# A conv, FFN and attention trunk in split fp32: nine of eleven down pairs by seven products, the closing tile by tile, weight sums outside the layers

## The chip, the cores and the metric

The kernel runs on one core of a Trainium2 chip, as one program. The metric is device time in microseconds. The profile times five engines: PE (matrix products), DVE and ACT (elementwise work), POOL (elementwise work, and the queue that issues accumulating DMAs) and SP (the queue of plain loads).

## The reference

512 tokens of width 1024 go through one short-convolution layer, a SwiGLU layer, one sliding-window attention layer on shared K and V, and a second SwiGLU layer; each part is normed on both sides and added to the residual stream. Everything is fp32. What matters here is the SwiGLU:

```python
D_FF = ((8 * D_MODEL // 3 + 255) // 256) * 256      # 2816
def rmsnorm(x, g):
    xf = x.astype(jnp.float32)
    r = lax.rsqrt(jnp.mean(xf * xf, axis=-1, keepdims=True) + EPS)
    return (xf * r).astype(x.dtype) * g
def swiglu(h, w_gate_up, w_down):
    g, u = jnp.split(h @ w_gate_up, 2, axis=-1)
    return (jax.nn.silu(g) * u) @ w_down
```

## The kernel before

**Products.** An fp32 product is made of three products of rounded parts: each operand is split into a high part (an ACT copy, `whi` or `ahi`) and the remainder (a DVE subtraction, `wlo` or `alo`), and `mm3` (L181 to L183) multiplies low by high, high by high and high by low. A `raw` tile holds a loaded weight until it is split.

**Seven products.** The 22 feature tiles of the SwiGLU make 11 pairs. A gate pair is computed by a seven-product scheme of the Strassen-Winograd kind (class `Gates`, jobs p = 1 to 7; tiles `gx`, `gy`, `gz`). The down projection has two forms. `ROUNDS` divides the feature tiles: the pairs of each round but the last go by seven products as well (`down_jobs`; tiles `px`, `py`, `pz`; the results gathered into `mix` by DVE at L1057), and the last round's tiles are multiplied directly in the closing (`unit`; tile `pmix`). Before, the rounds are tiles 0 to 6, 6 to 10, 10 to 14 and 14 to 22: seven pairs by seven products, eight tiles directly.

**Sums of weights.** Four of the seven products of a pair take sums of weight blocks (t1 to t4 in the code). They are made in DRAM (tiles `hsum`) by DMAs on POOL's queue: four copies, two accumulates, then one and one more, in four steps (class `Sums`). `sum_on` (issued at L588) starts a set at the place that `BEGIN` names, and carries every started set one step further at each later place: c0 to c7 are the eight column blocks of the convolution, 0f1 to 0p10 places of the first SwiGLU, a0 to a7 of the attention, 1f1 of the second SwiGLU. h00 to h11 are sums for the gates, d00 to d12 sets for the down rounds (layer, round). The program keeps these DMAs in written order on POOL's queue, and a step is issued only once what it reads has landed.

**POOL's other work** stands in the same queue: the cuts and multiplications of the convolution (L701, L712), accumulates of gate weights onto `raw` tiles (L442), and the reciprocal roots of the norms (`ur`: L281 for the norm behind a layer, L303 for the norm ahead of the next).

**Opening and closing.** A layer's result is normed token tile by token tile (128 tokens each): `take` (from PSUM; its square by ACT, `junk` L250), `mean` (`uv` L277, `ur` L281), `scale` (by the gain, L273), `update` of the residual `h` (L286), `square` (L294), `mean2` (L299, L303), `norm` (`xn`, L308, by ACT). PE then turns xn (`xt`, L319). `last_tile` does the rest for the fourth tile while PE begins the next layer's gates, and `keep` places splits of later weights between. The closing before runs in two halves: all four tiles for the output's first 512 columns (`first_half`), then for the others (`second_half`), with splits of following weights (`ahead`, L405 and L410) between.

**Order.** Where `manual_schedule` is on, the instructions of an engine stand in written order. `Line` serves the split weights to the products: it fetches into at most 7 raw tiles and keeps at most 5 split weights (`N_RAW`, `N_W`).

## Time and profile before

| | us |
|---|---|
| median of three runs | 1044.0 (1043.23 to 1045.44) |
| the profiled execution | 1043.19 |
| its span | 1041.4 |
| PE busy in it | 1024.6 |
| DVE busy | 754.0 |
| ACT busy | 555.7 |
| POOL busy | 194.3 |

A timeline row reads: start, duration, engine, line, operation, out<-in, shapes, count, and in brackets the idle time before it with what ended that. Listed durations of matmuls overlap; the distance between two starts is what one costs.

### The profile page before, as it was taken

How to read it: one execution, taken by the hardware profiler on the slowest of the kernel's cores; microseconds unless marked ns; L12 is line 12 of the kernel's file. 1: busy time of each engine (PE TensorE's matmuls, PEld its weight loads, DVE VectorE, ACT ScalarE, POOL GpSimd, SP SyncE). 2: the span in 40 equal slices, each digit the busy share in tenths (PEclk: the TensorE clock that was granted, in tenths of full speed). 3: DMA queues.
4: the chain of work that ended last, by engine and by line, in shares of the span. 5: the costliest groups of instructions: out<-in, count | busy, mean ns of one | idle time of the engine just before them, and what ended most of it. 6: DMA issues, size and time to landing. Idle time of an engine off the chain costs nothing.

```text
span 1041.4 us, 17098 instructions
## 1 busy us (share of the span) xinstructions
PE 1024.6 (98%) x6652; PEld 930.0 (89%) x6652; DVE 754.0 (72%) x1190; ACT 555.7 (53%) x947; POOL 194.3 (19%) x231
## 2 busy tenths in 40 slices
PE   9999999998999999999999999999999999999997
PEld 7888888998989898999898888889998999989986
DVE  5775655886767788666578999689786688786654
ACT  7222224864655455454474777678565555545531
POOL 0242202130121111220132542022110101011001
PEclk9999999999999999999999999999999999999999
DMA  9667775899889888998335674378988878888802
GB/s 330 262 165 229 197 218 138 207 263 262 271 205 264 226 208 256 235 244 274 136 122 144 138 202 122 104 201 206 269 253 225 196 216 188 219 200 204 236 28 81
DMA packets 63825, 212.05 MB, mean 204 GB/s; under 512 B 6912, under 2 KB 7808, under 8 KB 59136
## 3 DMA queue, kind: packets, MB, share of 16 engines
q0 software_dynamic: 17728, 81.80, 39.6%
q1 hardware_dynamic: 45440, 128.51, 35.0%
q8 instruction: 52, 0.85, 0.3%
q10 hardware_dynamic: 576, 0.66, 0.2%
q14 instruction: 29, 0.24, 0.1%
HBM read 204.64 MB, written 44.04 MB: 239 GB/s over the span
## 4 chain that ended last, share of the span: by engine, by line
PE 80%; DVE 8%; DMA 4%; issue 4%; ACT 3%; POOL 1%; POOLq 0%; DVEq 0%; SPq 0%; ACTq 0%
PE gx L181 6%; PE gx L182 6%; PE gx L183 6%; DMA raw<-in_w_gb_dram 4%; PE pmix L181 4%; PE pmix L182 4%; PE pmix L183 4%; PE gz L181 3%; PE gz L183 3%; PE gz L182 3%; PE px L181 2%; PE px L182 2%; PE px L183 2%; DVE wlo L476 2%; PE pcub L660 2%
## 5 line engine op out<-in xcount | busy, mean ns | idle before, releaser
L476 DVE TENSOR_TENSOR wlo<-raw,whi 128x1024 fp32r<-128x1024 f32 x209 | 253.9, 1218 | 106.7 <-ACT whi L469 105.9
L469 ACT ACTIVATE whi<-raw 128x1024 fp32r<-128x1024 f32 x209 | 218.1, 1052 | 179.9 <-DMA raw<-in_w_gb_dram 66.4
L442 POOL DMA_DIRECT2D raw<-in_w_gb_dram x84 | 73.3, 877 | 465.9 <-DVE wlo L476 245.6
L181 PE MATMUL gx<-xt,whi 128*128 128x256 f32 x528 | 150.7, 285 | 4.8 <-ACT gr L955 3.7
L182 PE MATMUL gx<-xt,whi 128*128 128x256 f32 x528 | 150.0, 284 | 0.0
L183 PE MATMUL gx<-xt,wlo 128*128 128x256 f32 x528 | 149.9, 284 | 0.0
L181 PEld LDWEIGHTS gx<-xt,whi 128*128 128x128 f32 x528 | 102.0, 193 | 6.0 <-ACT gr L955 4.4
L182 PEld LDWEIGHTS gx<-xt,whi 128*128 128x128 f32 x528 | 102.0, 193 | 0.0
L183 PEld LDWEIGHTS gx<-xt,wlo 128*128 128x128 f32 x528 | 102.0, 193 | 0.0
L176 ACT ACTIVATE whi<-raw 128x1024 fp32r<-128x1024 f32 x31 | 32.8, 1058 | 58.9 <-PE pu L182 25.0
L181 PE MATMUL pmix<-wlo,ahi 128*128 128x512 f32 (+1 forms) x136 | 51.3, 377 | 0.0
L182 PE MATMUL pmix<-whi,ahi 128*128 128x512 f32 (+1 forms) x136 | 51.2, 377 | 0.0
L183 PE MATMUL pmix<-whi,alo 128*128 128x512 f32 (+1 forms) x136 | 51.2, 377 | 0.0
L177 DVE TENSOR_TENSOR wlo<-raw,whi 128x1024 fp32r<-128x1024 f32 x31 | 47.4, 1528 | 4.8 <-ACT whi L176 4.5
L181 PE MATMUL gz<-xt,whi 128*128 128x256 f32 x176 | 49.9, 284 | 0.8 <-DVE gr L934 0.8
L181 PE MATMUL gx<-x,whi 128*128 128x256 f32 x176 | 50.1, 284 | 0.0
L181 PE MATMUL gy<-x,whi 128*128 128x256 f32 x176 | 50.0, 284 | 0.0
L182 PE MATMUL gz<-x,whi 128*128 128x256 f32 x176 | 49.8, 283 | 0.0
L181 PE MATMUL gz<-x,whi 128*128 128x256 f32 x176 | 49.8, 283 | 0.0
L183 PE MATMUL gz<-x,wlo 128*128 128x256 f32 x176 | 49.8, 283 | 0.0
L182 PE MATMUL gz<-xt,whi 128*128 128x256 f32 x176 | 49.8, 283 | 0.0
L182 PE MATMUL gy<-x,whi 128*128 128x256 f32 x176 | 49.8, 283 | 0.0
(279 smaller groups left out, 2954.5 us busy)
## 6 DMA issues: line engine op xcount, KB each, us to landing
raw<-in_w_gb_dram SPq DMA_DIRECT2D x92, 512.0 KB, 5.4
raw<-in_w_gb_dram POOLq DMA_DIRECT2D x84, 512.0 KB, 6.8
raw<-in_w_dn_dram SPq DMA_DIRECT2D x34, 512.0 KB, 5.7
raw<-hsum SPq DMA_DIRECT2D x28, 512.0 KB, 5.7
hsum<-in_w_dn_dram POOLq DMA_DIRECT2D x24, 512.0 KB, 7.2
raw<-in_w_in_dram SPq DMA_DIRECT2D x21, 512.0 KB, 6.9
hsum<-in_w_dn_dram POOLq DMA_DIRECT2D x12, 768.0 KB, 8.3
hsum<-in_w_gb_dram POOLq DMA_DIRECT2D x16, 512.0 KB, 7.0
```

The source lines that it names most:

```text
L176: nc.scalar.activation(hi, raw, AF.Copy)
L177: nc.vector.tensor_tensor(out=lo, in0=raw, in1=hi.bitcast(F32), op=ALU.subtract)
L181: nc.tensor.matmul(out, whi, xlo, start=start, stop=False, **kw)
L182: nc.tensor.matmul(out, whi, xhi, start=False, stop=False, **kw)
L183: nc.tensor.matmul(out, wlo, xhi, start=False, stop=stop, **kw)
L442: nc.gpsimd.dma_start(self.tile, self.jobs[0].more, accum_op=ALU.add))
L469: self.begun = nc.scalar.activation(hi[:, :n], raw, AF.Copy)
L476: nc.vector.tensor_tensor(out=lo[:, :n], in0=raw, in1=hi[:, :n].bitcast(F32), op=ALU.subtract)
L660: nc.tensor.matmul(ps, (whi, whi, wlo)[i][:, kk], (xhi, xlo, xhi)[i], start=k == i == 0, stop=k == KT - 1 and i == 2)
```

## The change

The rounds become tiles 0 to 6, 6 to 12, 12 to 18 and 18 to 22: nine pairs by seven products and four tiles directly. The sets of sums for the first SwiGLU start at c2, c4 and c6, those of the second at a1, a4 and a7, so that no set of the down rounds is made inside a SwiGLU layer (only h10 and h11 still are, from 0p10 on). In `down_jobs` all the products of one p follow each other, and a weight tile that serves two p is used by two `Part`s. The closing goes token tile by token tile: both halves of the columns, then scaling, mean and update of that tile, before the next; its weights are split into slots. Layer 1's opening uses a new `last_sum` and splits a third weight later; layer 0's `last_tile` places one more weight. In the attention's output the norm of tile t-1 stands before the second half of tile t, and the second SwiGLU's first weights are fetched one iteration earlier.

```diff
 KT = D // P
 F = 2816
 NF = F // P
-ROUNDS = [(0, 6), (6, 10), (10, 14), (14, 22)]
+ROUNDS = [(0, 6), (6, 12), (12, 18), (18, 22)]
 
 PAIRS = NF // 2
 
 BEGIN = {
-    "c0": ("h00", "h01"), "c4": ("d00",), "0f1": ("d01",), "0p3": ("d02",),
-    "0p7": ("h10", "h11"), "0p10": ("d10",), "a3": ("d11",), "1f1": ("d12",),
+    "c0": ("h00", "h01"), "c2": ("d00",), "c4": ("d01",), "c6": ("d02",),
+    "0p10": ("h10", "h11"), "a1": ("d10",), "a4": ("d11",), "a7": ("d12",),
 }
 PAIR = (1, 5, 6, 2, 7, 3, 4)
 SPLIT = {5: -2, 1: 0, 6: 2, 2: 3, 7: 4, 3: 6, 4: 8}
...
@@ -819,6 +835,7 @@
         res.update(3)
         splits(3)
         if keep:
+            keep()
             for i in range(2):
                 res.keep(0, 0, i)
                 res.keep(1, 0, i)
@@ -831,6 +848,29 @@
                 res.keep(2, 0, i)
         res.norm(3)
         splits(5)
+
+    def last_sum(res, then):
+        res.mean2(2)
+        res.scale(3, 0)
+        res.norm(2)
+        res.mean(3)
+        for f in range(4, 6):
+            res.split(0, f, 0)
+        res.scale(3, 1)
+        for f in range(6, 8):
+            res.split(0, f, 0)
+        res.update(3)
+        for b in range(2):
+            for i in range(2):
+                res.keep(b, 0, i)
+                if b:
+                    res.keep(3, 0, i, True)
+        res.square(3)
+        for i in range(2):
+            res.keep(2, 0, i)
+        then()
+        res.mean2(3)
+        res.norm(3)
 
     res = Update([wide("mix") for _ in range(NB)], B_CONV, [G_FPRE[0]], False)
     res.leaves = True
...
@@ -1012,22 +1052,17 @@
             b12, b11, b22, b21 = sums.blocks
             t1, t3, t2, t4 = sums.sums
             factor = {1: b11, 5: t1, 6: t2, 3: b22, 7: t3, 2: b21, 4: t4}
-            if len(cs) == 1:
-                order = [[(p, 0)] for p in (1, 5, 6, 3, 7, 2, 4)]
-            else:
-                order = [[(1, 0)], [(5, 0)], [(1, 1), (5, 1)], [(6, 0)], [(3, 0)],
-                         [(6, 1), (3, 1)], [(7, 0)], [(2, 0)], [(7, 1), (2, 1)], [(4, 0)],
-                         [(4, 1)]]
+            ps = (1, 5, 6, 3, 7, 2, 4)
+            order = [(p, c) for p in ps for c in range(len(cs))]
+            packed = [ps[i : i + 2] for i in range(0, len(ps), 2)]
             banks, left_of = {}, {p: len(kps) for p in factor}
             into = {1: (0, 0), 2: (0, 0), 6: (0, 1), 3: (0, 1), 5: (1, 1), 7: (1, 1), 4: (1, 0)}
             begun = set()
 
-            def run(parts):
+            def run(p, c, at=0):
                 def products(job):
-                    at = 0
...
@@ -1035,17 +1070,17 @@
                 opened = bs not in banks
                 if opened:
                     banks[bs] = [bank("p" + bs.lower(), POOLS[bs]) for _ in range(2)]
-                for n, k in enumerate(cs[c]):
-                    kk = slice(n * S, (n + 1) * S)
-                    left_of[p] -= 1
-                    for r in range(2):
+                left_of[p] -= len(cs[c])
+                i, half = into[p]
+                for r in range(2):
+                    for n, k in enumerate(cs[c]):
+                        kk = slice(n * S, (n + 1) * S)
                         ah, al = left(acts[k], p, r)
                         mm3(banks[bs][r], ah, al, hi[:, kk], lo[:, kk], opened and n == 0,
...
-                        run(parts)) for parts in order]
+            def rows(p, c):
+                return factor[p][cs[c][0] : cs[c][-1] + 1]
+
+            made = {}
+            for p in ps:
+                made[p, 0] = Job(Raw(rows(p, 0)), run(p, 0))
+            for both in packed if len(cs) > 1 else []:
+                job = Job(Raw(*(rows(p, 1) for p in both)))
+                for at, p in enumerate(both):
+                    made[p, 1] = Part(job, run(p, 1, at), at == len(both) - 1)
+            jobs = [made[at] for at in order]
             jobs[-1].then = then
-            for job in jobs[: None if len(cs) == 1 else -6]:
+            for job in jobs[: None if len(cs) == 1 else -8]:
                 job.alone = True
             return jobs
 
...
         def weights(half, j):
             return w_dn[l, half : 4 - half : 3 - 2 * half, f0 // 2 + j]
 
-        closing = [Job(Raw(weights(0, j))) for j in range(n // 2)]
-        key = {job: i + len(opening) for i, job in enumerate(jobs + closing)}
+        closing = [Job(Raw(weights(half, j))) for half in range(2) for j in range(n // 2)]
+        for job in closing:
...
                 if ks[-1] == 3:
                     line.done(gate.jobs[p])
 
-            for ks in ((0, 1), (2,), (3,)):
-                for gate in (a, b):
-                    multiply(gate, 1, ks)
-            a.take(1, True)
+            def start():
+                factors[1] = before.blocks(1)
+                for ks in ((0, 1), (2,), (3,)):
+                    for gate in (a, b):
+                        multiply(gate, 1, ks)
+                a.take(1, True)
+
+            if l:
+                last_sum(before, start)
+            else:
+                last_tile(before, [[(0, f)] for f in range(4, KT)] + [[], []], False, line.one)
+                start()
+            factors[2] = [x[0] for x in before.x[0][4:]]
             sum_on(f"{l}f0")
             for k in range(4):
                 multiply(a, 2, (k,))
-                if k in (0, 3):
+                if k in (l, 3):
                     for f in ((0, 1), (2, 3))[k // 3]:
                         before.turn(f, (2,))
             a.take(2)
             line.one()
-            line.one()
+            line.hi()
+            if l == 0:
+                line.lo()
             multiply(c, 1, (0, 1))
             for f in range(4):
                 before.turn(f, (3,))
...
             a.jobs[5].then = lambda: sum_on(f"{l}f3")
+            def wider():
+                line.limit = N_W
+
+            line.limit = N_W - l
+            c.jobs[2].then = lambda: (make(4), wider())[2:]
...
+        ws = [[job.w for job in closing[h * n // 2 : (h + 1) * n // 2]] for h in range(2)]
+        x = acts[-1]
         with tc.manual_schedule(engines=ALL):
+            if ahead:
+                ahead.one()
+                ahead.one()
             for t in range(NB):
-                if t < NB - 1:
-                    ps = bank("pmix")
-                    unit(ps, t, ws1, acts[-1], range(n), n)
+                end = t == NB - 1
+                ps = bank("pmix", ps_mm)
+                unit(ps, t, ws[0], x, range(n if t else n // 2), n)
+                if end and ahead:
+                    ps1 = bank("pmix", ps_mm)
+                    unit(ps1, t, ws[1], x, range(1), n)
+                    for b in range(4):
+                        res.turn(b, (0, 1))
+                if t == 0:
+                    ps1 = bank("pmix", ps_mm)
+                    unit(ps1, t, ws[1], x, range(n // 2), n)
+                    unit(ps, t, ws[0], x, range(n // 2, n), n)
+                if end and ahead:
+                    for f in range(4):
+                        res.split(0, f, 0)
+                    res.square(t - 1)
+                res.take(t, 0, ps)
+                if ahead and t:
+                    res.mean2(t - 1)
+                    if not end:
+                        ahead.lo()
+                    res.norm(t - 1)
+                if ahead:
+                    ps = ps1 if t == 0 or end else bank("pmix", ps_mm)
+                    unit(ps, t, ws[1], x, range(1 if end else 0 if t else n // 2, n), n)
                     res.take(t, 1, ps)
+                    res.scale(t, 0)
+                    if not end:
+                        res.mean(t)
+                        res.scale(t, 1)
+                        res.update(t)
+                        if t < NB - 2:
+                            res.square(t)
+                            ahead.hi()
+                    continue
+                if not end:
...
         for half in range(2):
             part(begun[half], 0, half, range(n - 1))
             ahead.one()
-            ahead.one()
-        for t in range(NB):
+        for t in range(NB - 1):
             for half in range(2):
-                if t == 0:
-                    ps = begun[half]
-                    part(ps, t, half, range(n - 1, n))
-                else:
-                    ps = bank("pmix", ps_mm)
-                    if (t, half) == (NB - 1, 1):
-                        part(ps, t, half, range(2))
-                        for b in range(4):
-                            res.turn(b, (0, 1))
-                        part(ps, t, half, range(2, n))
-                        for f in range(4):
-                            res.split(0, f, 0)
-                        res.square(NB - 2)
-                        res.take(t, 0, other)
-                    else:
-                        part(ps, t, half, range(n))
-                if (t, half) == (NB - 1, 0):
-                    other = ps
-                else:
-                    res.take(t, half, ps)
-            if t < NB - 1:
-                tile_done(res, t, square=t < NB - 2, more=ahead.slots if t == 2 else None)
+                ps = begun[half] if t == 0 else bank("pmix", ps_mm)
+                part(ps, t, half, range(n - 1 if t == 0 else 0, n))
+                res.take(t, half, ps)
+                if half == 0 and t > 0:
```

The POOL engine at the end of the convolution, before: the cut and product of the last column block (cut_1012, bry_1017), the two last accumulates of set d00 (hsum_136, hsum_137), a gate weight (raw_1327), and the first root of the layer's norm (ur_1140).

```order
L588 DMA hsum_134<-in_w_dn_dram 96x2048
L588 DMA hsum_135<-in_w_dn_dram 96x2048
L701 TENSOR_TENSOR cut_1012<-cru_1009 128x512
L712 TENSOR_TENSOR bry_1017<-cut_1012,bry_1017 128x512
L588 DMA hsum_136<-hsum_134 96x2048
L588 DMA hsum_137<-hsum_136 96x2048
L442 DMA raw_1327<-in_w_gb_dram 128x1024
L281 TENSOR_TENSOR ur_1140<-uv_1139,mhalf 128x1
```

The same engine and place now, from the last column block's accumulates on (its lines are a few later: L602 is before's L588, L443 L442, L282 L281):

```order
L602 DMA hsum_140<-hsum_138 96x2048
L602 DMA hsum_142<-in_w_dn_dram 96x2048
L602 DMA hsum_143<-in_w_dn_dram 96x2048
L602 DMA hsum_144<-in_w_dn_dram 96x2048
L602 DMA hsum_145<-in_w_dn_dram 96x2048
L602 DMA hsum_141<-hsum_140 96x2048
L602 DMA hsum_142<-in_w_dn_dram 96x2048
L602 DMA hsum_143<-in_w_dn_dram 96x2048
L602 DMA hsum_144<-hsum_142 96x2048
L602 DMA hsum_145<-hsum_144 96x2048
L443 DMA raw_1343<-in_w_gb_dram 128x1024
L282 TENSOR_TENSOR ur_1154<-uv_1153,mhalf 128x1
```

Sets d01 (hsum_138 to 141) and d02 (hsum_142 to 145) now stand ahead of the first root (ur_1154), with every one of their steps.

The DVE engine in the closing of layer 0, before, from the mean of the first token tile on (mix_2681, mix_2691 and mix_2683 are token tiles 0 to 2, h_4978 and h_4980 the residuals of tiles 0 and 1, wlo_5034 and wlo_5076 splits of following weights):

```order
L245 TENSOR_TENSOR mix_2681<-pmix_4992,mix_2681 128x512
L277 TENSOR_SCALAR uv_4818<-us_4817 128x1
L273 TENSOR_TENSOR mix_2681<-mix_2681,G_4820 128x512
L410 TENSOR_TENSOR wlo_5034<-raw_5021,whi_5033 128x1024
L286 SCALAR_TENSOR_TENSOR h_4978<-mix_2681,ur_4819,h_4978 128x1024
L245 TENSOR_TENSOR mix_2691<-pmix_5042,mix_2691 128x512
L299 TENSOR_SCALAR uv_4818<-us_4817 128x1
L277 TENSOR_SCALAR uv_4818<-us_4817 128x1
L273 TENSOR_TENSOR mix_2691<-mix_2691,G_4820 128x512
L286 SCALAR_TENSOR_TENSOR h_4980<-mix_2691,ur_4819,h_4980 128x1024
```

And now (lines one later; mix_2663 is token tile 0, mix_2693 token tile 1, h_4999 and h_5001 their residuals, wlo_5058 a split of a following weight):

```order
L274 TENSOR_TENSOR mix_2663<-mix_2663,G_4996 128x512
L287 SCALAR_TENSOR_TENSOR h_4999<-mix_2663,ur_4995,h_4999 128x1024
L246 TENSOR_TENSOR mix_2693<-pmix_5060,mix_2693 128x512
L300 TENSOR_SCALAR uv_4994<-us_4993 128x1
L411 TENSOR_TENSOR wlo_5058<-raw_5013,whi_5057 128x1024
L246 TENSOR_TENSOR mix_2693<-pmix_5082,mix_2693 128x512
L274 TENSOR_TENSOR mix_2693<-mix_2693,G_4996 128x512
L278 TENSOR_SCALAR uv_4994<-us_4993 128x1
L274 TENSOR_TENSOR mix_2693<-mix_2693,G_4996 128x512
L287 SCALAR_TENSOR_TENSOR h_5001<-mix_2693,ur_4995,h_5001 128x1024
```

A tile's second half was taken behind the update of the tile before; now both halves of a tile lie between two updates, and the split of the following weight stands between its two takes.

112 lines of the change are left out of this document (74 added, 38 removed).

## The prediction

> **What bounds the kernel now.** I read the page first (busy time, then the chain that ended last), then the timeline of PE around each break in its matmuls, then the POOL and DMA rows of the stages the change touches. The page:
>
> ```profile
> span 1041.4 us, 17098 instructions
> PE 1024.6 (98%) x6652; PEld 930.0 (89%) x6652; DVE 754.0 (72%) x1190; ACT 555.7 (53%) x947; POOL 194.3 (19%) x231
> ```
>
> PE is busy for 98% of the span. So time is saved here in two ways only: fewer matmuls, or fewer breaks between them. What a matmul costs is the distance between starts, since the listed durations overlap:
>
> ```profile
> 506.01 0.39 PE L183 MATMUL pmix<-whi,alo 128*128 128x512 f32 x1
> ...
> 519.61 0.39 PE L183 MATMUL pmix<-whi,alo 128*128 128x512 f32 x1
> 235.88 0.28 PE L181 MATMUL gx<-xt,whi 128*128 128x256 f32 x1
> ...
> 239.00 0.28 PE L183 MATMUL gx<-xt,wlo 128*128 128x256 f32 x1
> 242.07 0.58 PE L181 MATMUL gx<-xt,whi 128*128 128x256 f32 x1 [2.78 <-ACT gr L955]
> 242.45 0.41 PE L182 MATMUL gx<-xt,whi 128*128 128x256 f32 x1
> 242.66 0.41 PE L183 MATMUL gx<-xt,wlo 128*128 128x256 f32 x1
> 296.60 0.39 PE L183 MATMUL py<-whi,alo 128*128 128x512 f32 x1
> 297.32 0.50 PE L181 MATMUL px<-wlo,ahi 128*128 128x512 f32 x1 [0.34 <-DVE mix L1057]
> 750.61 0.28 PE L183 MATMUL gx<-xt,wlo 128*128 128x256 f32 x1
> 751.83 0.39 PE L181 MATMUL gx<-xt,whi 128*128 128x256 f32 x1 [0.94 <-ACT gr L955]
> 806.72 0.50 PE L181 MATMUL px<-wlo,ahi 128*128 128x512 f32 x1 [0.34 <-DVE mix L1057]
> ```
>
> From 506.01 to 519.61 lie 60 starts: 0.227 us per matmul of 512 columns. From 235.88 to 239.00 lie 26: 0.120 us for 256 columns. The breaks follow. At 239.00 the next start is 3.07 us later, 2.95 more than 0.120. At 296.60 it is 0.72 later, 0.5 more than 0.227, and the same bracket stands at 806.72. At 750.61 it is 1.22 later, 1.1 too much. After the break at 239 matmuls start 0.21 us apart (242.45, 242.66) with durations of 0.41: PE runs at half clock for a while. The window of that time, and one for later:
>
> ```profile
> 200.00:250.00 50.00, 47.02 (x379) 46.62 (x377) 41.00 (x56) 30.59 (x46) 11.36 (x15) 0.97 0.98 254
> 122.00:177.00 55.00, 55.00 (x244) 45.57 (x243) 28.85 (x39) 19.37 (x33) 6.27 (x8) 1.00 0.61 168
> ```
>
> The last three columns are granted clock, DMA share and GB/s. A clock of 0.97 over 50 us is 1.5 us lost, so the break at 239 costs 2.9 + 1.5 = 4.4 us. The DMA engines are 98% busy there: the second opening waits for weights.
>
> [...]
>
> **Part 1, matmuls removed.** Per layer the second and third rounds go from two pairs to three, and four feature tiles fewer are multiplied directly. Over both layers the instruction order has 180 closing matmuls of 512 columns and 24 of 256 fewer, and in exchange 96 on px, 24 on py and 48 on pz more, 168 of 512 columns. Net 12 x 0.227 + 24 x 0.120 = **-5.6 us**, certain, as PE is the bound in those stages.
>
> **Part 2, banks in the down products.** The breaks before px at 297.32 and 806.72 come from a bank that DVE still reads; six py matmuls (1.4 us) cover it. With all products of one p together, 18 py matmuls (4.1 us) stand there, in both layers. Both breaks go: 2 x 0.5 = **-1.0 us**.
>
> **Part 3, sums of the first layer moved ahead of its opening.** This is the doubtful part. Before, one set of three pairs is summed in the convolution; d01 and d02 follow inside the layer, in the stretch with DMA at 0.98. After, all three sets, of three pairs each (24 DMAs of 768 KB in place of 8), are issued before the layer's first root on POOL. POOL of before:
>
> ```profile
> 118.75 2.37 POOL L701 TENSOR_TENSOR cut<-cru 128x512 f32<-128x512 f32 x1 [8.02 <-ACT whi L176]
> 125.39 0.81 POOL L588 DMA_DIRECT2D hsum<-hsum  x1
> 132.78 0.79 POOL L588 DMA_DIRECT2D hsum<-hsum  x1 [6.58 <-issue]
> ...
> 168.52 0.57 POOL L281 TENSOR_TENSOR ur<-uv,mhalf 128x1 f32<-128x1 f32 x1 [17.98 <-DVE uv L277]
> ...
> q0 software_dynamic: 17728, 81.80, 39.6%
> q1 hardware_dynamic: 45440, 128.51, 35.0%
> ...
> hsum<-in_w_dn_dram POOLq DMA_DIRECT2D x12, 768.0 KB, 8.3
> ...
> hsum<-hsum POOLq DMA_DIRECT2D x4, 768.0 KB, 7.6
> ```
>
> Before, POOL stood idle for 18 us ahead of the first root at 168.52: there was room. After, the queue still has to issue nine accumulates and four copies from the sixth column block (c5) on, and the root stands behind the last of them. These steps begin at about 122, since the cut of the last block (118.75, 2.37 long, so ending at 121.1) now precedes them.
>
> Two ends follow. *Latency alone*: an accumulate waits for the landing of what it reads. From 122.4 the chain has four such waits (8.3, 7.6, 8.3, 7.6), so the last issue is at about 154 and the root is not late at all. *Throughput alone*: q0 moved 81.80 MB in 39.6% of 1041.4 us (412 us), and q1 128.51 MB in 364 us, 2.8 us a MB. If the 16.8 MB of copies in q0 (seven pairs in two layers and the gates' sums) cost as q1's, 47 us, the 65 MB of accumulates take 365 us, 5.6 us a MB. A 768 KB copy is then 2.2 us of all 16 engines and an accumulate 4.4. Eight accumulates and four copies must land before the ninth accumulate is issued: 8 x 4.4 + 4 x 2.2 = 44 us, so not before 166.4. Between 122 and 177 the engines are busy 0.61 x 55 = 33.6 us, of which two accumulates (125.39, 132.78) are 8.8; 24.8 us are other loads. If all of these are served first, the last issue is at 191. I take 177, a little short of halfway between 166.4 and 191 (10.6 us of loads): loads for later jobs run ahead only as buffers come free, so some can fall behind without harm. With the last issue itself (0.8, as at 125.39) the root comes at **177.8** in place of 168.5.
>
> [...]
>
> What a late root costs:
>
> ```profile
> 169.71 1.28 DVE L286 SCALAR_TENSOR_TENSOR h<-mix,ur,h 128x1024 f32<-128x1024 f32 x1
> 179.94 1.16 ACT L308 ACTIVATE xn<-h,ur 128x1024 f32<-128x1024 f32 x1 [0.52 <-POOL ur L303]
> 181.61 0.82 PE L319 MATMUL xt<-ident,xn 128*128 128x128 f32 x6
> ```
>
> From the root at 168.52 to the end of the second tile's xn (179.94 + 1.16 = 181.10) pass 12.6 us. PE turns that tile at 181.61, so there was half a microsecond to spare. A part of the 12.6 was waiting for PE's mixes, which are long done now; I take 12. The root at 177.8 puts the end of xn at 189.8 and PE's start some 0.2 later: PE idles 190.0 - 181.6 = **+8.4 us** and then runs at half clock, **+1.5** as at 239. Against this, the 4.4 us at 239 go: the sums of d01 and d02 (16 DMAs of 512 KB) leave the stretch whose DMA share is 0.98. **-4.4**. Sum of the opening: +5.5.
>
> **Part 4, closing of layer 0 tile by tile.** PE needs 24 x 0.227 = 5.45 us a tile, in both versions. The DVE and ACT rows of before give the parts of the new chain:
>
> ```profile
> 508.48 0.69 DVE L245 TENSOR_TENSOR mix<-pmix,mix 128x512 f32<-128x512 f32 x1 [3.20 <-PE pmix L183]
> 510.97 1.23 DVE L410 TENSOR_TENSOR wlo<-raw,whi 128x1024 fp32r<-128x1024 f32 x1
> 515.46 0.21 DVE L277 TENSOR_SCALAR uv<-us 128x1 f32<-128x1 f32 x1 [0.64 <-ACT junk L250]
> 516.71 1.29 DVE L286 SCALAR_TENSOR_TENSOR h<-mix,ur,h 128x1024 f32<-128x1024 f32 x1 [0.44 <-POOL ur L281]
> ...
> 509.26 0.63 ACT L250 ACTIVATE junk<-mix 128x512 f32<-128x512 f32 x1 [4.71 <-DVE mix L245]
> 509.89 1.04 ACT L405 ACTIVATE whi<-raw 128x1024 fp32r<-128x1024 f32 x1
> 513.48 1.06 ACT L294 ACTIVATE junk<-h 128x1024 f32<-128x1024 f32 x1 [2.55 <-DVE h L286]
> 514.45 0.19 ACT L294 ACTIVATION_READ_ACCUMULATOR junk<-h 128x1 f32 x1
> ```
>
> After, the split of a following weight lies inside the loop: update 1.29, square 1.06 + 0.19, whi 1.04, wlo 1.23 (now ahead of the take of the second half), take 0.69, junk 0.63 + 0.19, and 1.25 from uv to the next update: 7.6 us from one update to the next, against 5.45 of PE. The first update comes 2.75 us after its tile's matmuls (take, junk, uv to update), at 8.2 from the start; the second at 15.8; its square, the split and xn (1.29 + 1.25 + 1.04 + 1.16 and handoffs of 0.5) end at 21.0. PE asks for that tile's turn after three tiles and 15 matmuls, at 19.75. A wait of 1.3 there, and about 1.2 more where the low parts and the turn of the last two tiles follow the same chain: **+2.5 us** (0.5 if DVE overlaps more of it, 4 if each tile pays). Before had none.
>
> **Part 5, layer 1.** Its sums are made in the attention stage. The break at 750.61 is a whi behind a load on POOL:
>
> ```profile
> 742.88 0.86 POOL L442 DMA_DIRECT2D raw<-in_w_gb_dram  x1 [5.06 <-DMA hsum<-in_w_dn_dram]
> ```
>
> POOL issues it late, since it waits 5.06 us for a sum's landing. With the sums gone from there the 1.1 us go, and so, by the same earlier weights, two small breaks behind it (0.28 and 0.55 too much):
>
> ```profile
> 771.96 0.28 PE L183 MATMUL gy<-x,wlo 128*128 128x256 f32 x1
> 772.36 0.39 PE L181 MATMUL gx<-xt,whi 128*128 128x256 f32 x1
> 778.10 0.28 PE L183 MATMUL gz<-x,wlo 128*128 128x256 f32 x1
> 778.77 0.36 PE L181 MATMUL gx<-xt,whi 128*128 128x256 f32 x1 [0.39 <-DVE st L934]
> ```
>
> Together **-1.9** (0 if they only move). The reordered opening moves PE's wait for xn but its DVE work is not less, so I count it at nothing (-1 to +1). In the closing of layer 1 a tile's DVE work (two takes, two scalings, an update: 4 x 0.69 + 1.29 + 0.21) stays under PE's 5.45; only the last tile gets an update of half rows more, **+0.3** (0 to 0.5).
>
> **Sum**: -5.6 - 1.0 + 5.5 + 2.5 - 1.9 + 0.3 = -0.2 us on the profiled run's 1043.19 (span 1041.4 and 1.8 around it), which lies 0.8 below the median of 1044.0. I forecast **1043.0 us**.
>
> **Rivals.** *Faster: the root is in time.* For it speak the latency end (154) and POOL's 18 us of idle time; against it the 44 us of engine time that have to fit in 46 (122.4 to 168.5) beside the loads. Then the opening gives -4.4 instead of +5.5: 1043.0 - 9.9 = 1033.1; a root a few microseconds late lies between. *Slower: plain loads take their full share.* For it speaks the DMA share of 0.61 there without the added sums, against it that loads ahead of their use can slip. The last issue is then at 191 in place of 177 and PE waits up to 14 us more: 1057; with half of that, 1050. It decides from a root later than 181 (3.1 us more, over 1046.1). *The closing chain overlaps in full*, since three tiles let DVE and ACT catch up: 1040.5. *It does not do what it says*: the loads, not the sums, filled the engines at 239, and that break stays: 1047.4.
>
> **How the numbers follow.** Forecast, with its own range of 1040.5 to 1046.1: 0.48. Root in time or nearly (1031 to 1040.5): 0.32. Loads take their share: 0.13. Break at 239 stays: 0.07. About 0.2% can be told from no change, 1041.9 to 1046.1. Of the forecast's 0.48, some 0.13 lie under 1041.9 (there the closing overlaps) and 0.02 at its upper edge: faster 0.45, same 0.33, slower 0.22. The range leaves out a tenth at each end: 1033 to 1051.
>
> **What would show it.** The first root of POOL behind the sums near 178, PE's gap ahead of the first turn of xt near 8 us and none at 239; no bracket on px; in the closing of layer 0 xt waiting for xn by 1 to 2 us; no bracket near 750. A root before 169, or a gap at 239 that stays, would prove the sum of the opening wrong.

## The result, and the profile after

| | before | after |
|---|---|---|
| median, us | 1043.62 (4 runs, 1041.8 to 1045.44) | 1060.07 (4 runs, 1058.81 to 1061.6) |
| ratio | 1 | 1.0158 (95% interval 1.0145 to 1.0172) |
| span of the profiled run, us | 1041.4 | 1059.8 |

The change costs 16.5 us. The forecast was 1043.0 with a range up to 1051. The page of the changed kernel begins:

```profile
span 1059.8 us, 17129 instructions
PE 1023.1 (97%) x6616; PEld 927.0 (87%) x6616; DVE 767.3 (72%) x1225; ACT 566.8 (53%) x964; POOL 194.8 (18%) x231
```

PE works less and the span is 18.4 us longer: breaks have come in. I took the distance of every start of a matmul to the next from both traces, less what is usual for that width (0.227, 0.120 and 0.109 us), and summed it by stage. A stretch at half clock (granted clock 0.50, as from 704.19 to 709.50 in the changed kernel) counts as a break.

| stage | before | after | difference | predicted |
|---|---|---|---|---|
| first opening (175 to 250) | 5.2 | 12.0 | +6.8 | +5.5 |
| gates of layer 0, to the closing (250 to 525; px at 296 taken out) | 0.3 | 3.3 | +3.0 | 0 |
| closing of layer 0 and behind it (525 to 550) | 0.2 | 4.6 | +4.4 | +2.5 |
| attention (550 to 700) | 3.2 | 4.5 | +1.3 | 0 |
| second opening and behind it (700 to 800) | 4.1 | 12.8 | +8.7 | -1.9 |
| px breaks, and the rest behind 800 | 1.4 | 0 | -1.4 | -1.0 |
| behind the last matmul | 7.2 | 8.4 | +1.2 | +0.3 |
| matmuls | | | -5.6 | -5.6 |

These add up to 18.4, the difference of the spans. Most of it lies behind two stretches in which the DMA engines are now nearly or wholly full; the run without accumulates, below, shows that the sums are the cause there. The windows of the changed kernel (last three columns: granted clock, DMA share, GB/s):

```profile
122.00:177.00 55.00, 55.00 (x244) 45.58 (x243) 25.53 (x35) 15.17 (x27) 10.22 (x13) 1.00 1.01 282
590.00:680.00 90.00, 88.08 (x601) 74.94 (x600) 80.82 (x248) 65.94 (x194) 39.71 (x40) 1.00 0.92 255
650.00:670.00 20.00, 20.00 (x145) 16.81 (x144) 18.35 (x58) 15.49 (x48) 5.98 (x8) 1.00 0.70 176
```

The first stood at 0.61 before. The third is a part of the second: even there the engines had some idle time (a share of 0.70). The second before:

```profile
590.00:680.00 90.00, 89.42 (x587) 76.53 (x587) 78.37 (x223) 63.37 (x178) 29.65 (x28) 1.00 0.56 145
```

POOL's timeline of the changed kernel ahead of the first root, and PE at the first turns:

```profile
150.73 0.80 POOL L602 DMA_DIRECT2D hsum<-in_w_dn_dram  x1 [2.38 <-DMA hsum<-in_w_dn_dram]
168.01 0.79 POOL L602 DMA_DIRECT2D hsum<-hsum  x1 [16.49 <-DMA hsum<-in_w_dn_dram]
177.62 0.79 POOL L602 DMA_DIRECT2D hsum<-hsum  x1 [8.82 <-DMA hsum<-hsum]
...
178.85 1.08 POOL L282 TENSOR_TENSOR ur<-uv,mhalf 128x1 f32<-128x1 f32 x1
...
181.35 0.39 PE L184 MATMUL pmix<-whi,ylo 128*128 128x512 f32 x1
185.86 0.48 PE L320 MATMUL xt<-ident,xn 128*128 128x128 f32 x1 [4.12 <-ACT xn L309]
191.18 1.12 PE L320 MATMUL xt<-ident,xn 128*128 128x128 f32 x4 [4.85 <-ACT xn L309]
```

The last accumulate is issued at 177.62 (177 was forecast) and the root comes at 178.85 (177.8). PE breaks twice, for each tile's xn. The same picture, unforeseen, stands at the end of the attention. Before, the first root there stood on POOL at 679.71, and the last DMA of sums ahead of it at 644.65:

```profile
679.71 0.93 POOL L281 TENSOR_TENSOR ur<-uv,mhalf 128x1 f32<-128x1 f32 x1
```

As changed (POOL, then DVE, then PE):

```profile
666.88 0.82 POOL L602 DMA_DIRECT2D hsum<-hsum  x1 [8.61 <-DMA hsum<-hsum]
...
677.30 0.81 POOL L602 DMA_DIRECT2D hsum<-in_w_dn_dram  x1 [7.56 <-DMA hsum<-in_w_dn_dram]
679.62 0.81 POOL L602 DMA_DIRECT2D hsum<-in_w_dn_dram  x1 [1.51 <-DMA hsum<-in_w_dn_dram]
680.30 1.03 POOL L443 DMA_DIRECT2D raw<-in_w_gb_dram  x1
697.62 0.86 POOL L443 DMA_DIRECT2D raw<-in_w_gb_dram  x1 [16.29 <-DMA raw<-in_w_gb_dram]
...
701.33 0.89 POOL L282 TENSOR_TENSOR ur<-uv,mhalf 128x1 f32<-128x1 f32 x1
...
702.25 1.28 DVE L287 SCALAR_TENSOR_TENSOR h<-mixo,ur,h 128x1024 f32<-128x1024 f32 x1 [10.30 <-POOL ur L282]
...
700.03 0.39 PE L184 MATMUL pmix<-whi,olo 128*128 128x512 f32 x1
704.19 0.79 PE L182 MATMUL pmix<-wlo,ohi 128*128 128x512 f32 x1 [3.77 <-DVE mixo L246]
...
710.88 0.27 PE L320 MATMUL xt<-ident,xn 128*128 128x128 f32 x1
713.27 0.33 PE L320 MATMUL xt<-ident,xn 128*128 128x128 f32 x1 [2.12 <-ACT xn L309]
```

Read it backward: PE waits for DVE's take, which stands behind the update; DVE waited 10.30 us for the root; the root stands on POOL behind an accumulate of a gate weight, and that waited 16.29 us for its plain load, in DMA engines that are full (a share of 1.02 to 1.03 from 680 to 700). The landing times say the same: in the view of DMA issues the median of the `hsum<-in_w_dn_dram` DMAs of 768 KB has gone from 8.3 to 13.4 us:

```profile
hsum<-in_w_dn_dram POOLq DMA_DIRECT2D x36, 768.0 KB, 13.4
```

### The profile page after: what moved, and what is told of

The parts are those of the page before. It is cut to its first block, busy times and chain, and to the rows that moved or that the text cites. A ratio compares the mean times of both kernels' runs of the same rounds, so it can differ in the third digit from the quotient of the medians.

```text
span 1059.8 us, 17129 instructions
## 1 busy us (share of the span) xinstructions
PE 1023.1 (97%) x6616; PEld 927.0 (87%) x6616; DVE 767.3 (72%) x1225; ACT 566.8 (53%) x964; POOL 194.8 (18%) x231
## 3 DMA queue, kind: packets, MB, share of 16 engines
q0 software_dynamic: 18752, 90.19, 41.5%
## 4 chain that ended last, share of the span: by engine, by line
PE 73%; DMA 9%; DVE 8%; issue 4%; ACT 4%; POOL 2%; POOLq 0%; DVEq 0%; SPq 0%; ACTq 0%
PE gx L182 7%; PE gx L183 7%; PE gx L184 7%; DMA raw<-in_w_gb_dram 3%; PE gz L184 3%; PE gz L183 3%; PE gz L182 3%; DMA hsum<-in_w_dn_dram 3%; PE px L182 3%; PE px L183 3%; PE px L184 3%; DMA hsum<-hsum 2%; PE pcub L674 2%; PE gy L182 2%; PE gy L184 2%
## 5 line engine op out<-in xcount | busy, mean ns | idle before, releaser
L470 ACT ACTIVATE whi<-raw 128x1024 fp32r<-128x1024 f32 x217 | 225.6, 1046 | 195.7 <-DMA raw<-in_w_gb_dram 47.3
L443 POOL DMA_DIRECT2D raw<-in_w_gb_dram x84 | 73.5, 890 | 522.4 <-DVE wlo L477 350.9
L177 ACT ACTIVATE whi<-raw 128x1024 fp32r<-128x1024 f32 x31 | 32.8, 1058 | 60.4 <-PE pu L183 24.5
L184 PE MATMUL gy<-x,wlo 128*128 128x256 f32 x176 | 49.9, 283 | 1.5 <-DVE wlo L477 1.5
L184 PE MATMUL gz<-xt,wlo 128*128 128x256 f32 x176 | 49.8, 283 | 0.0
L184 PE MATMUL gx<-x,wlo 128*128 128x256 f32 x176 | 49.8, 283 | 0.0
## 6 DMA issues: line engine op xcount, KB each, us to landing
hsum<-in_w_dn_dram POOLq DMA_DIRECT2D x36, 768.0 KB, 13.4
```

Of the source, the lines that this page charges most:

```text
L177: nc.scalar.activation(hi, raw, AF.Copy)
L184: nc.tensor.matmul(out, wlo, xhi, start=False, stop=stop, **kw)
L443: nc.gpsimd.dma_start(self.tile, self.jobs[0].more, accum_op=ALU.add))
L470: self.begun = nc.scalar.activation(hi[:, :n], raw, AF.Copy)
```

## The experiments

All are made from the changed kernel unless said otherwise, and timed against the kernel before.

### Where the sums stand (four runs)

The first question was whether the places of the sums are at fault. Four kernels differ from the changed one in `BEGIN` alone. The first has all places of before:

```diff
-    "c0": ("h00", "h01"), "c2": ("d00",), "c4": ("d01",), "c6": ("d02",),
-    "0p10": ("h10", "h11"), "a1": ("d10",), "a4": ("d11",), "a7": ("d12",),
+    "c0": ("h00", "h01"), "c4": ("d00",), "0f1": ("d01",), "0p3": ("d02",),
+    "0p7": ("h10", "h11"), "0p10": ("d10",), "a3": ("d11",), "1f1": ("d12",),
```

The second has the first of these lines alone, the third the second alone, and the fourth moves the last set only:

```diff
-    "0p10": ("h10", "h11"), "a1": ("d10",), "a4": ("d11",), "a7": ("d12",),
+    "0p10": ("h10", "h11"), "a1": ("d10",), "a4": ("d11",), "1f1": ("d12",),
```

> The changed kernel with every set of sums started at the places of the kernel before (d00 c4, d01 0f1, d02 0p3, h10 and h11 0p7, d10 0p10, d11 a3, d12 1f1); rounds, products and closing as changed. Theory: the sums ahead of the norms' roots on POOL cost 6.8 us in the first opening (11.98 of breaks between 175 and 250 against 5.21 before) and 9.4 us around the second (12.84 between 700 and 775 against 3.48): 1060 - 16 = 1044 us, with the break of 3 us of the second opening's weights near 239 back. Rival: plain loads that start earlier, and the new order of the attention's output, make the second root late: it stays late here too, and the time is 1051 to 1054.

Measured: 1073.05 us, ratio 1.0287 (1.026 to 1.0314).

> Only the first SwiGLU's sums (d00, d01, d02) at the places of before, the second's as changed. Theory: only the first opening's 6.8 us go, about 1053 us; the break of some 4 us and a half-clock stretch in the attention's output stay. Rival: the queue of the convolution also feeds delays behind it, so more than 6.8 us go.

Measured: 1068.13 us, 1.0222 (1.0181 to 1.0262).

> Only the second SwiGLU's sums (h10, h11, d10, d11, d12) at the places of before, the first's as changed. Theory: the 9.4 us between 700 and 775 go, less a break of 1.1 us as before behind a gate weight that waits for a sum, and 1 us in the attention: about 1051 us. Rival (early plain loads): the first root of the second layer stays over 10 us late, 1058 to 1060.

Measured: 1065.37 us, 1.0207 (1.0185 to 1.0228).

> As changed but for the last set alone: d12 starts in the second layer (1f1) and not at the end of the attention (a7). Theory: d12's copies and two accumulates (667 to 680) are what fills the DMA engines ahead of the root at 701; without them the root is at about 685 and the 9.4 us go: about 1051 us, as with all of the layer's sets moved. Rival (d10 and d11 in the attention, or early plain loads): under 3 us go, 1057 to 1060.

Measured: 1061.67 us, 1.0174 (1.0154 to 1.0194).

All four expectations failed on the time, theory and rival alike: no set gains by going back. The breaks moved as the theory said, but they only moved. With d12 later, the 9.5 us of breaks between 700 and 725 shrink to 0.7, and 12.8 us come between 725 and 775 in place of 3.3, where a gate product now waits 4.37 us for ACT (the second row). PE of the run with the last set later:

```profile
764.70 0.28 PE L184 MATMUL gx<-xt,wlo 128*128 128x256 f32 x1
769.34 0.39 PE L182 MATMUL gx<-xt,whi 128*128 128x256 f32 x1 [4.37 <-ACT gr L995]
```

With the first layer's sets at the places of before, the breaks of 175 to 200 go from 11 to 1.3, and 9 to 10 us come between 225 and 250 and 3 to 6 behind 325. So the question became whether the sums' amount or their order is paid.

### No accumulates

This kernel leaves out every accumulate of the down rounds' sets; their first copies stay.

```diff
+    for sum_name, one_sum in sums_of.items():
+        if sum_name[0] == "d":
+            del one_sum.steps[1:]
```

> As changed, with all accumulates of the down sets left out (only their first copies are made, so the seven-product down projections multiply unsummed weights). Theory (the sums' DMA work is what the change pays): the breaks at both openings go (11.98 between 175 and 250, 12.84 between 700 and 775, less than 2 left in each) and 1.5 to 3 of the attention's: 1034 to 1038. Rival (the layer-1 plain loads fetched earlier and the attention's new order): the break around 700 keeps over 5 us: 1041 or more.

Measured: 1042.27 us, ratio 0.9981 (0.9964 to 0.9997), 17.8 us less than the changed kernel. Both roots are early. POOL of this run:

```profile
166.88 0.57 POOL L282 TENSOR_TENSOR ur<-uv,mhalf 128x1 f32<-128x1 f32 x1 [18.30 <-DVE uv L278]
677.37 0.90 POOL L282 TENSOR_TENSOR ur<-uv,mhalf 128x1 f32<-128x1 f32 x1
```

In the first opening 1.3 us of breaks are left, between 700 and 775 3.2, so the early plain loads and the new order of the attention's output are not what made the root late. The accumulates are the price. This edit takes away both their DMA time and the waits that they put into POOL's queue, so it doesn't tell these two apart. The time is 4 us over the 1034 to 1038 expected; it lies where the rival had it, but without the break of over 5 us around 700 that the rival named. The last matmul starts at 1029.4 (before 1034.2, as changed 1051.4), but the span ends only at 1041.0, 6 us behind the last output's issue at 1034.5 (3 us as changed); why stays open.

### Order: two accumulates behind the roots

The last two accumulates of d02 are not issued ahead of the first root but in the layer.

```diff
-    sum_on("o0")
     issue(len(issues))
 ...
-    sum_on("o1")
-    issue(len(issues))
```

> As changed, but the last two accumulates of set d02 (issued at 168.01 and 177.62 on POOL, ahead of the first root at 178.85) are issued inside the layer, behind all the roots of its first norm. Theory (POOL's queue in order): the root is ready at about 169 as before, the 11 us of breaks between 175 and 200 go, and two accumulates of 4.4 us in the stretch of the opening cost at most 4: 1053 to 1056 against 1060. Rival (the DMA engines are simply full): the gate weights of the opening come late instead, and over 8 us of the 11 come back between 200 and 275: 1057 to 1061.

Measured: 1057.25 us, 1.0136 (1.0114 to 1.0157), in the rival's range. The root is at 166.94 as the theory had it, and 11 us of breaks become 4.0; but 4.9 come back between 225 and 250, behind the two accumulates that now stand at 206.58 and 217.22. Of the 7 us that go at the root, 4.9 thus come back; the time is 2.8 us less than the changed kernel's.

### The rounds alone

In the kernel before:

```diff
-ROUNDS = [(0, 6), (6, 10), (10, 14), (14, 22)]
+ROUNDS = [(0, 6), (6, 12), (12, 18), (18, 22)]
```

> The kernel before with the changed rounds alone (nine pairs by seven products, four tiles directly): its places of the sums, its closing in halves, its order of the down products. PE has the same 5.6 us less. Theory (the DMA work of the two added pairs' sums and accumulates is paid by the opening and by the gates behind it): the break at 239 grows from 4.4 to 9, gates at 320 to 340 wait for 3 to 5, the second layer alike; 1056 to 1066. Rival (sums are free as long as no root stands behind them): 1037 to 1042.

Measured: 1074.89 us, 1.0315 (1.0293 to 1.0337), worse than the theory's 1056 to 1066. PE of this run:

```profile
237.60 0.28 PE L183 MATMUL gx<-xt,wlo 128*128 128x256 f32 x1
245.79 0.58 PE L181 MATMUL gx<-xt,whi 128*128 128x256 f32 x1 [7.91 <-ACT gr L955]
534.41 0.39 PE L183 MATMUL pmix<-whi,alo 128*128 128x512 f32 x1
536.73 0.33 PE L319 MATMUL xt<-ident,xn 128*128 128x128 f32 x1 [1.93 <-ACT xn L308]
541.66 1.76 PE L319 MATMUL xt<-ident,xn 128*128 128x128 f32 x7 [4.60 <-ACT xn L308]
```

So in the kernel before the two added pairs cost 32 us. Not all of that is the sums: the old closing, in halves, has 8.5 us of breaks between 525 and 550 (the last three rows; before 0.2), since four tiles give PE less work to cover it. The other parts of the change win nearly half of the 32 us back. The first of the four runs above had the other parts with the sums at the places of before, and took 1073.05, the same within the noise; so nearly all that is won back, some 13 us, comes from moving the sums.

### Eight pairs

```diff
-ROUNDS = [(0, 6), (6, 12), (12, 18), (18, 22)]
+ROUNDS = [(0, 6), (6, 12), (12, 16), (16, 22)]
```

> As changed, with eight pairs by seven products and six feature tiles directly (rounds 0 to 6, 6 to 12, 12 to 16, 16 to 22). PE has 6 matmuls of 512 columns and 12 of 256 more, +2.8 us. Theory (the last set's DMA work makes both roots late): d02 and d12 are a third smaller, 512 KB in place of 768 a DMA, and about 6 of the 26 us of engine time of each go: breaks at 175 and 700 shrink by 4 to 6 us each: 1051 to 1056. Rival (the order and not the amount): +2.8, 1062 to 1063.

Measured: 1046.32 us, 1.0027 (1.0012 to 1.0041), under the theory's range. One pair less in d02 makes the root come at 171.73 instead of 178.85, and the breaks of the whole run go from 42.2 to 24.4 us. Some 14 of the difference lie at the two openings, 4 in the closing, where six tiles give PE more work (next section).

### The split inside the closing's chain

```diff
                 if ahead and t:
                     res.mean2(t - 1)
-                    if not end:
-                        ahead.lo()
                     res.norm(t - 1)
 ...
                         res.update(t)
+                        if t:
+                            ahead.lo()
                         if t < NB - 2:
```

> As changed, but in the closing of layer 0 the low part of the following weight is made behind the tile's update instead of between its two takes. Theory (my chain from update to update, 7.4 us measured, holds the subtraction of 1.23 and the wait of 0.8 for its high part): the chain shrinks to 5.5 to 6, and of the 4.6 us of breaks between 525 and 551 some 2 to 3 go: 1057 to 1058. Rival (PE waits there for the last tile alone): under 0.5 go.

Measured: 1061.54 us, 1.0178 (1.0154 to 1.0202): the theory of the split fell. Breaks of 5.0 us are left between 525 and 550, so none went, as the rival had it. DVE of the changed kernel from update to update, then of this run, then of the run with eight pairs:

```profile
517.77 1.29 DVE L287 SCALAR_TENSOR_TENSOR h<-mix,ur,h 128x1024 f32<-128x1024 f32 x1 [0.46 <-POOL ur L282]
...
525.21 1.28 DVE L287 SCALAR_TENSOR_TENSOR h<-mix,ur,h 128x1024 f32<-128x1024 f32 x1 [0.43 <-POOL ur L282]
```

```profile
515.69 1.28 DVE L287 SCALAR_TENSOR_TENSOR h<-mix,ur,h 128x1024 f32<-128x1024 f32 x1 [0.46 <-POOL ur L282]
...
522.72 1.29 DVE L287 SCALAR_TENSOR_TENSOR h<-mix,ur,h 128x1024 f32<-128x1024 f32 x1 [0.43 <-POOL ur L282]
```

```profile
511.38 1.29 DVE L287 SCALAR_TENSOR_TENSOR h<-mix,ur,h 128x1024 f32<-128x1024 f32 x1 [0.44 <-POOL ur L282]
...
519.55 1.28 DVE L287 SCALAR_TENSOR_TENSOR h<-mix,ur,h 128x1024 f32<-128x1024 f32 x1 [0.44 <-POOL ur L282]
```

The period is 7.44 us as changed (7.6 was forecast), 7.03 with the subtraction behind the update, and 8.17 with eight pairs, which is PE's own 36 x 0.227 for six feature tiles. With six tiles the closing's breaks are 0.4 us in place of 4.6. What sets the period with four tiles is thus more than the subtraction: with it out of the chain another one is right behind, on ACT, which between two updates has the square, the split's high part, two squares of takes and xn (without a gap from 517.07 to 521.44). It needs 7.03, far from PE's 5.45.

### One step earlier (three runs)

```diff
-    "c0": ("h00", "h01"), "c2": ("d00",), "c4": ("d01",), "c6": ("d02",),
-    "0p10": ("h10", "h11"), "a1": ("d10",), "a4": ("d11",), "a7": ("d12",),
+    "c0": ("h00", "h01"), "c1": ("d00",), "c3": ("d01",), "c5": ("d02",),
+    "0p10": ("h10", "h11"), "a0": ("d10",), "a3": ("d11",), "a6": ("d12",),
```

The second run has this with eight pairs. The third, with eight pairs too, has another line for the second layer:

```diff
+    "0p7": ("h10", "h11"), "0p10": ("d10",), "a2": ("d11",), "a5": ("d12",),
```

> As changed, with the down sets' sums started one step earlier each (c1, c3, c5 and a0, a3, a6): 16 us earlier in the convolution, 12 in the attention. Theory (roots late behind the sums on POOL, and DMA time to be had earlier): both roots come in time or under 3 us late, the breaks of 11 and 9.5 shrink to 3 each: 1045 to 1049. Rival (the DMA engines are full over the whole stretch, 1.00 and above from 590 to 710): the root of the second layer stays over 5 us late: 1052 to 1057.

Measured: 1053.17 us, 1.011 (1.0086 to 1.0135).

> Eight of eleven pairs by seven products, and the down sets' sums one step earlier (c1, c3, c5, a0, a3, a6). Theory: of the 4.5 us of breaks at 175 and the 6.8 between 675 and 750 some 3 and 3 go: 1039 to 1042, under the kernel before. Rival: the sums only shift, 1045 to 1048.

Measured: 1049.56 us, 1.007 (1.0055 to 1.0085).

> Eight of eleven pairs; sums at c1, c3, c5 as in the run with eight pairs and steps earlier, but the second layer's gate sums from 0p7 on and its down sets from 0p10, a2 and a5 on, so that they end sooner still. Theory: the break at the second root goes, but the sums of the gates then meet the gate loads of the first layer's end (DMA share 0.93 there before), 1 to 4 us of breaks between 450 and 500: 1039 to 1044. Rival: over 5 us there, 1046 or more.

Measured: 1050.96 us, 1.0094 (1.007 to 1.0117).

The roots come nearly in time (172.68 and 690.58 with nine pairs, in place of 178.85 and 701.33), but PE now breaks ahead of them: 9.1 us up to 175 in place of 4.9, and 8.2 between 600 and 625 in place of 3.5. With nine pairs (POOL, DVE and PE, first in the convolution, then POOL and PE in the attention):

```profile
127.65 0.80 POOL L602 DMA_DIRECT2D hsum<-hsum  x1 [8.18 <-DMA hsum<-in_w_dn_dram]
...
130.25 1.57 POOL L715 TENSOR_TENSOR cut<-cru 128x512 f32<-128x512 f32 x1
145.62 1.61 POOL L726 TENSOR_TENSOR bry<-cut,bry 128x512 f32<-128x512 f32 x1 [13.81 <-DVE cut L720]
...
142.48 0.48 DVE L716 TENSOR_SCALAR cut<-cut,gt 128x512 f32<-128x512 f32 x1
...
148.68 0.50 PE L184 MATMUL pmix<-whi,ylo 128*128 128x512 f32 x1
152.03 0.50 PE L182 MATMUL pmix<-wlo,yhi 128*128 128x512 f32 x1 [2.86 <-ACT yhi L728]
...
599.29 0.81 POOL L602 DMA_DIRECT2D hsum<-hsum  x1 [4.44 <-DVE ra L1340]
599.83 1.58 POOL L1341 TENSOR_TENSOR sh<-sh,stab 128x512 f32<-128x512 f32 x1
...
601.73 0.39 PE L184 MATMUL pq<-xhi,wlo 128*128 128x512 f32 x1
605.73 0.55 PE L1400 MATMUL psc<-rlo,rhi 64*128 64x256 f32 x1 [3.60 <-DVE nm L1412]
```

Waiting accumulates on POOL are a part of this, but not all of it. In the convolution POOL's cut of the seventh block stands at 130.25 behind an accumulate that waited 8.18 us (as changed it stood at 118.72). DVE, though, takes that cut up at 142.48 only, late in its own order, and POOL waits 13.81 us for DVE. In the attention a multiplication of the ropes (position factors, `sh`) stands behind an accumulate, but what it reads came from DVE less than 1 us before. Why DVE's work falls so late in these runs is not shown.

Eight pairs lose by the step (1049.56 against 1046.32), and the third run has 8.1 us of breaks between 475 and 500, where its gate sums now stand. All three times lie where the rivals had them or above: with nine pairs at 1053, though not with a root over 5 us late as the rival had it; nor are the engines full from 590 to 710 throughout, as it also had it (0.70 between 650 and 670 as changed).

### Amount or order: the same places with nine and with eight pairs

Only the sets ahead of a root go one step earlier, so that less of POOL's other work stands behind them.

```diff
-    "c0": ("h00", "h01"), "c2": ("d00",), "c4": ("d01",), "c6": ("d02",),
-    "0p10": ("h10", "h11"), "a1": ("d10",), "a4": ("d11",), "a7": ("d12",),
+    "c0": ("h00", "h01"), "c2": ("d00",), "c4": ("d01",), "c5": ("d02",),
+    "0p10": ("h10", "h11"), "a1": ("d10",), "a3": ("d11",), "a6": ("d12",),
```

One run has this with nine pairs, one with eight. A third, with eight pairs, keeps c6 for d02 and issues its last accumulate behind the roots:

```diff
-    sum_on("o1")
-    issue(len(issues))
```

> Nine pairs as changed, with d02 one step earlier (c5), d11 and d12 one step earlier (a3, a6), d00, d01 and d10 as changed. Theory (order): breaks at 175 to 225 3 to 6 us in place of 12, at 700 to 750 4 to 6 in place of 12.4, at 600 3 to 4: 1045 to 1050. Rival (amount): the nine accumulates and four copies need their time all the same, and the roots stay over 6 us late: 1053 to 1058.

Measured: 1054.87 us, 1.0119 (1.0099 to 1.0138).

> Eight pairs with the places of the nine-pair run beside it (c2, c4, c5, a1, a3, a6), no accumulate behind the roots. Theory: one pair less in d02 and d12 takes 8.7 us of engine time out of each stretch ahead of a root, so both roots are in time and the breaks there are under 2 us each: 1039 to 1043. Rival (amount): 1045 to 1048.

Measured: 1041.27 us, 0.999 (0.9975 to 1.0005).

> Eight of eleven pairs by seven products. First layer: places as changed (c2, c4, c6), the very last accumulate of d02 issued behind the roots. Second layer: only the later two sets one step earlier (a1, a3, a6), d10 as changed, so that the ropes that stood behind d10's accumulates (3.8 and 1.1 us at 601 and 620 one step earlier) are left alone. Theory (what stands behind a waiting accumulate in POOL's order is what is paid): breaks at 175 to 225 under 3 us (4.5 in the eight-pair run), at 675 to 750 under 4 (6.8), at 600 about 2: 1040 to 1043, at or just under the kernel before. Rival (the amount of DMA work is paid wherever it stands): 1045 to 1048.

Measured: 1040.81 us, 0.9981 (0.9967 to 0.9994): faster than both kernels, if only by 0.2% than the kernel before.

POOL at the first root with nine pairs, then with eight, at the same places:

```profile
175.50 0.79 POOL L602 DMA_DIRECT2D hsum<-hsum  x1 [13.41 <-DMA hsum<-hsum]
...
176.73 1.08 POOL L282 TENSOR_TENSOR ur<-uv,mhalf 128x1 f32<-128x1 f32 x1
```

```profile
166.60 0.77 POOL L602 DMA_DIRECT2D hsum<-hsum  x1 [10.29 <-DMA raw<-in_w_gb_dram]
...
168.42 0.57 POOL L282 TENSOR_TENSOR ur<-uv,mhalf 128x1 f32<-128x1 f32 x1
```

With nine pairs, d02 a whole step of the convolution earlier gains 2 us at the root (176.73 against 178.85). With one pair less at the same places the last accumulate is issued 8.9 us sooner, about the 8.7 that a pair's share was worked out to. At this root, and at these places, the amount thus weighs more than the place. It does not decide alone: with all three sets a step earlier, the same nine pairs lost 10.4 us up to 250, the convolution's breaks counted, against 16.9 as changed. At the second root the place counts too: the same nine pairs bring that root from 701.33 to 694.04, and the breaks of 700 to 750 from 12.4 to 6.0.

| | places as changed | last sets a step earlier |
|---|---|---|
| nine pairs, us | 1060.07 | 1054.87 |
| eight pairs, us | 1046.32 | 1041.27 |

Of the expectations, the rival (amount) had the time right with nine pairs, the theories with eight. The four times together say more than each theory: by the ratios the step gains about 4 us with nine pairs and with eight, and a pair less about 13.5 at either place, its shorter sums, its closing and its added matmuls together. So amount and place are both paid, side by side. The third run adds nothing clear to the second (1040.81 against 1041.27).

## Why the prediction was wrong, point by point

- **Part 1, fewer matmuls** (-5.6): right; PE has 12 matmuls of 512 columns and 24 of 256 fewer.
- **Part 2, banks** (-1.0): right; nothing between the down products waits any more.
- **Part 3, first opening** (+5.5): the mechanism was right and the place of the root within 1.1 us (178.85 against 177.8). That it came so near has luck in it: 177 was picked between 166.4 and 191, and the price of 4.4 us for an accumulate was too high (3.8, under Part 5). The size was off by 1.3: there are two breaks, 4.3 and 5.2 us long, and the granted clock was 0.50 from 184.5 to 194.0, over the end of the first and the whole second. The break at 239 is gone, as forecast. Of the two ends the late one (191) was too late, and the early one (154) far off. The late end was my estimate for the case that all other loads are served first; the last issue came at 177.62, with the engines full (1.01 from 122 to 177). Between 122 and 180 SP's queue waited 40.6 us in all for DVE's `wlo` ahead of its loads into raw tiles (L436). So loads that were held back by their buffers can be the reason; that they are is not shown. The rival "the loads fill the engines at 239" was refuted; the break there comes and goes with the sums (4.4 before, none after, 10 with the rounds alone).
- **Part 4, closing** (+2.5): the chain was right (7.44 us against 7.6, row by row) and the first wait too (1.24 us at 529.04 against 1.3). What was mis-sized is what follows it: three breaks of 0.6 to 1.0 us and some small ones, 3.4 us together, in place of 1.2. The run with eight pairs shows the condition (the chain is hidden where PE needs longer than it).
- **Part 5, layer 1** (-1.9): **the step that failed.** The part said that the sums "are made in the attention stage" and counted only what they free in the layer. It never asked what Part 3 had asked: how much DMA time the attention has, what stands behind the accumulates on POOL, and when the next root is due. Before, POOL issued 9 DMAs of sums between 583 and 700 (one of 768 KB, eight of 512 KB); after, 23 of 768 KB and four for the gates. By the prediction's estimates, 2.2 us for a copy of 768 KB and 4.4 for an accumulate, three sets are 3 x 26.4 = 79 us, and the gates' sums come on top. The stage had 40 us free between 590 and 680 (0.44 of 90), and before's 9 DMAs, some 22 us by the same prices, made room: 62 us for over 79. The run without accumulates gives a lower price: with the 24 accumulates the POOL queue's packets (q0 on the page) took 41.5% of 1059.8 us, without them 33.5% of 1041.0, an estimated 3.8 us for each. That makes it 59 us for 72, still too little. The windows of that stage before would have told it in advance, and were not set against the sums. In the sum Part 5 is +8.7 instead of -1.9, and +1.3 in the attention itself: 12 of the 18.6 us between the sum and the profiled spans. Of the 8.7, the accumulates are the cause: without them 700 to 800 has 3.2 us of breaks, 0.9 less than before. The run with the last set later (breaks of 700 to 725 gone) and the one with nine pairs a step earlier fit this. Full engines are not all of it: from 650 to 670 their share was 0.70, while POOL waited 8.61 us for one accumulate to land before it issued the next copies (666.88). So the steps' order has a part as well, and how much is not shown. Part 5 also put the reordered opening at nothing (-1 to +1). Of the 3.2 us left without accumulates, 1.7 are its own: PE waits for DVE's low part (740 as changed) in every run with the new opening, and in neither run with the old one.
- **Terms that were not in the sum**: +3.0 in the gates of layer 0 (1.6 us at 319, the rest at 499 and 505), of which only the place is known, not the cause (without accumulates the break at 319 is 0.3, but 2.1 us in all are left there); +0.9 at the very end, where DVE now scales the first half ahead of the two last takes. The early loads of layer 1 were not tried alone.
- **Rivals and range.** The rival of plain loads that take their full share had a price of 1057, near the result, but by a first root at 191 that did not come. The range ended at 1051, since a second late root was no case in it. The sum was also added to the profiled run's 1043.19 and not to the median of 1044.0, which is 0.8 us of the miss.

## What to carry to other kernels

When work is moved out of a full stage into a free one, budget the stage that receives it as strictly as the one it leaves: its idle DMA time against the moved DMA time, and the first thing due behind it on the issuing queue. A price that was worked out once for one layer belongs to every layer that gets the same edit. Moving the last sets by a step gained about as much with nine pairs as with eight, but it did not make up for the amount: with nine pairs no place that was tried came below the kernel before.

## What the hardware showed that I had not expected

After two breaks PE stayed at half clock (granted clock 0.50) for different times. At 242 in the kernel before, behind 2.8 us of idle time, it took 2.9 us (242.07 to 245.01, matmuls 0.21 apart); at 704 in the changed kernel, behind 3.8 us of idle time, 5.3 us (704.19 to 709.50):

```profile
704.78 0.63 PE L183 MATMUL pmix<-whi,ohi 128*128 128x512 f32 x1
705.21 0.63 PE L184 MATMUL pmix<-whi,olo 128*128 128x512 f32 x1
...
709.48 0.43 PE L182 MATMUL pmix<-wlo,ohi 128*128 128x512 f32 x1
709.74 0.39 PE L183 MATMUL pmix<-whi,ohi 128*128 128x512 f32 x1
```

Starts lie 0.43 us apart up to 709.48, 0.2 more than usual over 13 matmuls, 2.6 us lost. With the break of 3.9 us ahead of them that makes 6.5.
